# Four of the eight late modulation blocks moved into the feature stage of a planned one-core diffusion step, and the order of all engines set anew

## The chip, the cores and the metric

The kernel runs on one core of one Trainium2 chip. The metric is the device time of one execution in microseconds. It is taken as the median of several runs; lower is better.

## The reference

The reference is one inference step of one layer. 1024 latent tokens and 128 context tokens of width 1024 are normalised and modulated, projected once, and sent through two token mixers (HGRN2 with 4 heads of 128, RWKV-7 with 8 heads of 64, both in both directions). The results are joined, projected and added; then comes a gated feed-forward part with a depthwise convolution.

```python
mod = jax.nn.silu(c) @ ada_w[l] + ada_b[l]            # 6 sections of 1024, for c and for c_ctx
shift1, scale1, gate1, shift2, scale2, gate2 = jnp.split(mod[:, None, :], 6, axis=-1)
h = rmsnorm(x, p['norm_mix_w']) * (1 + scale1) + shift1
u = h @ p['w_in']
o_a, s_hgrn_new = hgrn2_mixer(u[..., :P_A], ...)
o_b, s_rwkv_new = rwkv7_mixer(u[..., P_A:], ...)
x = x + gate1 * (jnp.concatenate([o_a, o_b], axis=-1) @ p['w_out'])
h = rmsnorm(x, p['norm_ffn_w']) * (1 + scale2) + shift2
gt = ffn_conv_fn(h @ p['ffn_w_gate']) + p['ffn_conv_b']
x = x + gate2 * ((jax.nn.gelu(gt) * (h @ p['ffn_w_up'])) @ p['ffn_w_down'])
```

What matters here is `mod`: a product of two rows (c and c_ctx) with a 1024 x 6144 matrix, 25 MB to load for little arithmetic. `shift1` and `scale1` are needed at once. `gate1`, `shift2`, `scale2` and `gate2`, columns 2048 to 6143, are needed only after the mixers. Scans that depend on every earlier token (RWKV-7) are computed in chunks of 64 tokens; a chunk needs the inverse of a triangular 64 x 64 system.

## The kernel before, in words

**Recording and planning.** The kernel does not issue its instructions as it is written. The class `Plan` records every operation (an `Op`: one instruction, or a group kept together) with what it reads and writes, and in `schedule` sets one order for TensorE (PE), VectorE (DVE), ScalarE (ACT), GpSimd (POOL) and SyncE (SP, which issues the loads; stores go to SP or POOL, whichever the plan picks). At each step it takes, for the engine that is free first, the ready operation with the highest rank: the length of the work that hangs on it (`tail`) plus a lead. Leads come from the table `LEADS` by the function that recorded the operation, and from `with plan.ahead(...)`. On PE a change between the split-precision matmuls (mode `f32r`) and all others costs rank (`INTO`, `OUT`, `SWITCH`). Costs of operations and transfers (`pe_cost`, `wire`) are numbers in the code. Places in memory are given out with the order: a tile's buffers are used in turn, and tiles that share a place (`near`) follow each other in the order of the program. Each engine and each queue then runs its list in order, so an instruction that waits holds up all behind it.

**Stages.** (1) The input is loaded, normalised and transposed; `mod_columns` makes `shift1` and `scale1`; the first two column blocks are projected (L1253 to L1255). (2) The feature stage: `conv_rkv` projects blocks of 128 columns by `proj` (each product is a triple of `f32r` matmuls, L1098 to L1100, of 128 x 384), `features` makes the chunk matrices of one of four head pairs, and `elim` inverts the triangular systems on DVE, 31 steps of two instructions (L1478, L1481), then fills them up with small matmuls (L1497, L1506). It runs five times, for the four pairs and for the context. Its buffers are `asys`, `tsys` (loaded with identities, L1472), `etmp`, `ttd` and `tn`. (3) The chain stage: `chains` runs 18 dependent chunk steps for each of two groups of heads (loads at L1727 and L1729, values at L1736 and L1737, products at L1746, L1790, L1797, L1805 to L1818); `hgrn_block` (L1601 to L1662) and `hgrn_out` (L1692 to L1707) work beside them, the rest of the projections too, and toward its end the loads of the output weights (L1939) begin. (4) `wo_tile` (L1981 to L1983), (5) the feed-forward front (L2090), and (6) its second product `ffn_down` (L2239 to L2241).

**The modulation blocks.** `ada_block(b)`, b from 0 to 7, makes 512 columns: a bias row (L995), eight loads of 128 x 512 (256 KB each, L1002), for each load four matmuls with 32 columns of the stationary side (L1005; four more for the bias at L999), a copy (L1006), a store for blocks 0, 1 (`gate1`, read again by `gate_rows` before stage 4) and 6, 7 (`gate2`, read at stage 6), and a transpose (L1013). Blocks 2, 3 are `shift2` and 4, 5 `scale2`, needed in stage 4. The weights go through two buffers `adaw2`; all eight blocks are recorded in the loop over the chain steps, one for two steps, with the lead `LEAD_ADA`, the last two with 700.

In the profile an ordinary fp32 matmul leaves two records: one block has 64 at L1005, 8 at L999 and 1 at L1013.

Of the kernel before, what the change touches and what calls it, by code (L numbers as in the profile page):

```python
# [20 lines left out]
P = 128  # L21
# [10 lines left out]
NLATE = 5  # L32
FILL = (1, 1, 1)
STRETCH = 2.76
LEAD_ADA = -9.0
LATE = 1.2
SWITCH = 2.0
INTO = 3.22
OUT = 2.0
HAM = 3.413  # L40
QUIET = 0.65
BUSY = 200.0
LEADS = {'hgrn_block': -10.8, 'hgrn_out': 89.1, 'ada_block': 34.8, 'prep': 35.0, 'mod_scale': 90, 'const': 103.8, 'params': -82, 'param_loads': -0.4, 'wo_tile': 8.1, 'ffn_down': -27.1, 'chains': -3.8, 'hgrn_in': 0.0, 'features': 0.0, 'elim': -12.5, 'post': 22.1, 'conv_rkv': 0.0, 'bonus_rows': -40.6, 'turned': 0.0, 'step_kernel': 0.0}


C_W0, C_A0, C_KK, C_KA, C_RK, C_LNW, C_LNB = 0, 8, 12, 16, 20, 24, 28
# [125 lines left out]
class Plan:  # L172
# [147 lines left out]
    def close(self, forms, room=()):  # L320
        op = Op()
        op.id, op.forms, op.deps, op.succ, op.after = len(self.ops), forms, set(), [], []
        self.ops.append(op)
        reads, writes, op.tiles = [], [], set()
        for m, a, k, _ in forms[0][1]:
            w, r = self.operands(m, a, k)
            writes += w
            reads += r
        for ap in reads + writes + list(room):
            if ap.offset >> self.BITS:  # L330
                op.tiles.add(ap.offset >> self.BITS)
# [12 lines left out]

        todo = []
        for k, reg, whole in each(reads, False):
            ws, rs = self.live.setdefault(k, ([], []))
            for w in ws:
                if overlap(w[0], reg):
                    op.deps.add(w[1])  # L350
            todo.append((rs, reg))
        for k, reg, whole in each(writes, True):
            ws, rs = self.live.setdefault(k, ([], []))
            for l in (ws, rs):
                keep = []
# [12 lines left out]
        if self.first is not None:  # L368
            op.deps.add(self.first)
        for v in op.tiles:  # L370
            self.tiles[v][3] += 1
        op.place, op.dense, op.lead, op.kind = None, False, self.lead + LEADS.get(self.kind, 0.0), self.kind
# [107 lines left out]
    def wire(self, a):  # L480

        def run(x):
            r = 1
            for s, c in reversed(list(x.ap)[1:]):
                if c > 1 and s != r:
                    break
                r *= c
            return r
        total = a[0].ap[0][1] * self.count(a[0])
        piece = min(run(a[0]), run(a[1]), 16384)  # L490
        return total / piece * (.007 + .0371e-3 * 4 * piece) / 16 + .01

    @staticmethod
    def pe_cost(l):
        busy = [[0.0] * 4 for _ in range(4)]
        issue, mode = 0.0, None
        for m, a, k, _ in l:
            out, lhsT, rhs = a[0], a[1], a[2]
            q = lambda ap: ((ap.offset & Plan.LOW) // ap.ap[0][0]) // 32
            span = lambda n: 1 if n <= 32 else 2 if n <= 64 else 4  # L500
            if m == "transpose":
                rows, cols, r0, c0, t = span(lhsT.ap[0][1]), 4, q(lhsT), 0, .0048 + .00081 * Plan.count(lhsT)
            else:
                rows, cols, r0, c0 = span(lhsT.ap[0][1]), span(Plan.count(lhsT)), q(lhsT), q(out)
                n = Plan.count(rhs)
                if lhsT.dtype == F32R:
                    t = (n + 32) / 2400
                else:
                    t = 2 * max(.098 if cols == 4 else .052, .005 + .00083 * n)
            cells = [(i, j) for i in range(r0, min(4, r0 + rows)) for j in range(c0, min(4, c0 + cols))]  # L510
# [20 lines left out]
    def schedule(self):  # L531
# [106 lines left out]
        while done < len(ops):  # L638
# [54 lines left out]
            c = op.cost[e]  # L693
            if e == "PE":
                if mode is not None and op.mode != mode:
                    c += .12 if op.mode == "f32r" else .09
                mode = op.mode
                w = int(t / HAM)
                if area.get(w - 1, 0.0) < .4 * HAM:
                    c *= 1.9  # L700
                for v in range(w, int((t + c) / HAM) + 1):
                    area[v] = area.get(v, 0.0) + op.area * (min(t + c, (v + 1) * HAM) - max(t, v * HAM)) / c
                recent.append((t, t + c, op.area))
# [91 lines left out]
def step_kernel(ctx: ExitStack, tc: tile.TileContext, I, O):  # L795
# [52 lines left out]
    def banks(name, first, count, each=1, free=False):  # L848
# [17 lines left out]
        .add("kb", 768, 2).add("vt", 384, 2) \  # L866
        .add("ako", 1024).add("asys", 1024).add("tsys", 1024).add("etmp", 256).add("ttd", 1024) \
        .add("tn", 1024)
    Layout(fx, 0, NX).add("tt", 2048).add("wlora", 512).add("ha", 384, 2).add("hb", 384, 2)
    v0 = plan.tags["rkv"].places[0][1]  # L870
    plan.tag("sgt", [(low, v0 + 3 * T)], T)
# [66 lines left out]
    def pbank(tag="pj"):  # L938
        return tl(tag, [P, 512])
# [50 lines left out]

    def ada_block(b):

        c0 = 2048 + 512 * b
        br = tl("adab", [4, P])
        ld(br, I["ada_b"][0, c0:c0 + 512].rearrange("(a b) -> a b", b=P))  # L995
        ps, mr = pbank("a"), tl("adam", [P, P])
        with plan.together(mr):
            for q in range(4):
                mm(ps[32 * q:32 * q + 32, 0:P], one[:, q, :], br, True, False)  # L999
        for kt in range(KT):  # L1000
            w = tl("adaw2", [P, 512])
            ld(w, I["ada_w"][0, kt * P:(kt + 1) * P, c0:c0 + 512])  # L1002
            with plan.together():
                for q in range(4):
                    mm(ps[32 * q:32 * q + 32, 0:P], sT[:, kt, :], w[:, P * q:P * q + P], False, kt == KT - 1)  # L1005
# [6 lines left out]
        pq = pbank("a")  # L1012
        pe.transpose(pq[:, 0:P], mr, ident)  # L1013
# [533 lines left out]
    def conv_rkv(p, j):  # L1547
        t = tl("rkv", [P, T])
        conv_tiles((2560 + j * 512 + p * P, 4 * j + p, t))
        return t  # L1550

    kv = [conv_rkv(0, 1), conv_rkv(0, 2)]
    for p in range(NPAIR):
        k, v = kv
# [326 lines left out]
    def post(i, oh, ol, early):  # L1881
# [23 lines left out]
                pe.transpose(ps[:, p * P:(p + 1) * P], y[:, p * P:(p + 1) * P], ident)  # L1905
        split(oh[:, 4:8], ol[:, 4:8], ps.rearrange("p (k t) -> p k t", k=4))

    cg = [chains(0), chains(1)]
    rest = [(hgrn_block, h, tb) for h in range(4) for tb in range(3)]
    for n in range(NCH + 1):  # L1910
        for g in range(2):
            next(cg[g], None)
        if n % 2 == 0 and n:
            if n // 2 <= 8:
                with plan.ahead(700.0 if n // 2 > 6 else LEAD_ADA):
                    ada_block(n // 2 - 1)
        if n % 2 and n // 2 < NT:
            bonus_rows(n // 2)
# [416 lines left out]
```

## Time and profile before

| | |
|---|---|
| median of 3 runs | 1864.29 us (1860.72 to 1865.18) |
| profiled execution | 1861.02 us, its span 1859.2 us, mean granted clock of TensorE 0.989 |
| busy, share of the span | PE 96%, weight loads of PE 86%, DVE 76%, ACT 47%, POOL 16% |
| moved by the DMA queues | 307 MB, 165 GB/s over the span |

The span is cut below into stretches by the first matmul of a stage: the chains' first (L1746) starts at 535.4 us, the feed-forward front's first (L2090) close to 1071 us. A busy PE is not one at its peak, since ends of matmuls are modelled; so the idle time before an instruction and what ended it are read beside the busy share.

### The profile page before, as it was taken

To read this page: it belongs to the slowest core of one execution; us is meant where nothing else is said; L and a number is where in the kernel's file an instruction comes from. 1 tells how busy PE (TensorE), PEld (TensorE's weight loads), DVE (VectorE), ACT (ScalarE), POOL (GpSimd) and SP (SyncE) were. 2 spreads that over 40 slices of the span, in tenths; PEclk is the share of its full clock that TensorE was granted. 3 is DMA by queue.
4 is the path that set the end of the run, shared out by engine and by line. 5 is a ranking of instruction groups with operands and counts; after the bars stand their busy time and mean duration, and the time that the engine had idled before them with its cause. 6 is when DMAs were issued, how large, how long until landed. Compare 5 with 4: busy or idle time off the path is not lost.

```text
span 1859.2 us, 45181 instructions
## 1 busy us (share of the span) xinstructions
PE 1790.9 (96%) x18369; PEld 1602.7 (86%) x18369; DVE 1409.0 (76%) x2643; ACT 870.2 (47%) x1766; POOL 295.9 (16%) x565
## 2 busy tenths in 40 slices
PE   7999999999999998999899989999999999999998
PEld 4989888889987887888778889999999999887886
DVE  7659898977747787787787789999999954886443
ACT  6556666643235564655435854444444333422321
POOL 2113425353211221222100100000000000000000
PEclk9999999999999999999899989999999999999999
DMA  9325637486567678877977612222222246675351
GB/s 322 100 76 141 151 97 193 108 229 182 170 199 233 200 217 242 245 230 244 301 232 249 222 54 72 82 72 72 72 72 72 83 140 213 237 245 190 125 165 62
DMA packets 268927, 307.44 MB, mean 165 GB/s; under 512 B 62339, under 2 KB 213153, under 8 KB 268720
## 3 DMA queue, kind: packets, MB, share of 16 engines
q1 hardware_dynamic: 241568, 222.17, 40.4%
q0 software_dynamic: 27152, 82.40, 13.1%
q8 instruction: 144, 2.36, 0.5%
q14 instruction: 63, 0.52, 0.1%
HBM read 200.50 MB, written 103.99 MB: 164 GB/s over the span
## 4 chain that ended last, share of the span: by engine, by line
PE 69%; DMA 4%; DVE 2%; issue 1%; ACT 1%; ACTq 0%; DVEq 0%; SPq 0%
PE banks L2090 27%; PE banks L2239 5%; PE banks L2240 5%; PE banks L2241 5%; PE banks L1098 3%; PE banks L1099 3%; PE banks L1100 3%; PE banks L1746 2%; PE banks L1981 2%; PE banks L1983 2%; PE banks L1982 2%; DMA top<-in_ada_w_dram 2%; DMA low<-d_ak 1%; PE banks L1816 1%; PE banks L1790 1%
## 5 line engine op out<-in xcount | busy, mean ns | idle before, releaser
L1098 PE MATMUL banks<-hh,wh 128*128 128x384 f32 x768 | 278.3, 362 | 0.0
L1099 PE MATMUL banks<-hl,wh 128*128 128x384 f32 x768 | 258.3, 336 | 0.7 <-issue 0.7
L1100 PE MATMUL banks<-hh,wl 128*128 128x384 f32 x768 | 258.5, 337 | 0.0
L2179 DVE SCALAR_TENSOR_TENSOR low<-low,pf 128x1024 f32<-128x1024 f32 x176 | 224.7, 1278 | 6.8 <-ACT low L2173 5.3
L2090 PE MATMUL banks<-qm,wh 128*128 128x320 f32 x968 | 224.3, 311 | 0.0
L2090 PE MATMUL banks<-qm,wl 128*128 128x320 f32 x528 | 163.8, 310 | 2.3 <-DVE wl L2060 2.3
L2090 PE MATMUL banks<-hbm,wh 128*128 128x256 f32 x880 | 162.4, 282 | 0.0
L2090 PEld LDWEIGHTS banks<-qm,wh 128*128 128x128 f32 x968 | 162.2, 190 | 0.1
L1098 PEld LDWEIGHTS banks<-hh,wh 128*128 128x128 f32 x768 | 144.9, 189 | 19.6 <-issue 12.9
L1099 PEld LDWEIGHTS banks<-hl,wh 128*128 128x128 f32 x768 | 145.4, 189 | 3.3 <-issue 2.2
L1100 PEld LDWEIGHTS banks<-hh,wl 128*128 128x128 f32 x768 | 144.9, 189 | 0.0
L2090 PEld LDWEIGHTS banks<-hbm,wh 128*128 128x128 f32 x880 | 139.5, 190 | 0.0
L2090 PE MATMUL banks<-ham,wh 128*128 128x256 f32 (+1 forms) x616 | 133.3, 297 | 3.3 <-ACT ham L2023 2.5
L2090 PE MATMUL banks<-hbm,wl 128*128 128x256 f32 x440 | 124.3, 283 | 0.0
L2090 PEld LDWEIGHTS banks<-ham,wh 128*128 128x128 f32 x616 | 102.8, 192 | 3.7 <-ACT ham L2023 2.8
L2090 PEld LDWEIGHTS banks<-qm,wl 128*128 128x128 f32 x528 | 99.6, 189 | 2.6 <-DVE wl L2060 2.6
L2060 ACT CAST wh<-fx 128x512 fp32r<-128x512 f32 x88 | 54.5, 621 | 82.2 <-PE banks L2090 72.5
L2128 ACT COPY fx<-banks 128x320 f32<-128x320 f32 (+1 forms) x132 | 52.4, 397 | 81.7 <-PE banks L2090 81.4
L2239 PE MATMUL banks<-qm,hbm 128*128 128x512 f32 x216 | 85.5, 396 | 0.0
L2240 PE MATMUL banks<-qm,hbm 128*128 128x512 f32 x216 | 85.5, 396 | 0.0
L2241 PE MATMUL banks<-qm,hbm 128*128 128x512 f32 x216 | 85.4, 395 | 0.0
L2090 PEld LDWEIGHTS banks<-hbm,wl 128*128 128x128 f32 x440 | 84.0, 191 | 0.0
(510 smaller groups left out, 4368.8 us busy)
## 6 DMA issues: line engine op xcount, KB each, us to landing
wr<-in_w_in_dram SPq DMA_DIRECT2D x34, 512.0 KB
top<-in_ada_w_dram SPq DMA_DIRECT2D x64, 256.0 KB
low<-d_ak SPq DMA_DIRECT2D x64, 192.0 KB
d_a<-low POOLq DMA_DIRECT2D x21, 576.0 KB, 3.5
low<-in_ffn_w_up_dram SPq DMA_DIRECT2D x22, 512.0 KB
wr<-in_ffn_w_gate_dram SPq DMA_DIRECT2D x22, 512.0 KB
low<-d_kb SPq DMA_DIRECT2D x36, 256.0 KB
low<-d_a SPq DMA_DIRECT2D x12, 704.0 KB
```

The lines of the kernel that those rows point to most:

```text
L1098: mm(o, wh[:, kt, :], hh[:, kt, c], kt == 0, False)
L1099: mm(o, wh[:, kt, :], hl[:, kt, c], False, False)
L1100: mm(o, wl[:, kt, :], hh[:, kt, c], False, kt == KT - 1)
L1746: mm(pa[h][:, P * w:P * w + P], kb[hc[h], w, :], W[hc[h], A0[h] + 192 * w:A0[h] + 192 * w + P], True, True)
L1981: mm(ps, oh[:, kt, :], woh, kt == 0, False)
L2060: split(*w, src)
L2090: pe.matmul(o, a[:, kt, :], b[:, kt, :], start=start and first, stop=last, skip_group_check=not start)
L2128: act.copy(keep[n], y[:, 0:w])
L2179: dve.scalar_tensor_tensor(av, shifted(dy, dx), tap(3 * dy + dx), av, MUL, ADD)
L2239: mm(o, lh, w[:, 0, c], first, False)
L2240: mm(o, lh, w[:, 1, c], False, False)
L2241: mm(o, ll, w[:, 0, c], False, last)
```

## The change

Blocks 4 to 7 are recorded ahead of the feature stage, with buffers of their own: six for the weights in the places of `ttd`, `tn` and `tsys`, the bias row and the copy in that of `etmp`, and the PSUM banks `el` of the eliminations. Blocks 0 to 3 stay in the loop over the chain steps, with their two buffers. The planner's prices of transfers and of mode changes, its leads and the ranks `INTO`, `OUT` and `BUSY` are other numbers, and a table `NUDGE` adds a number to the lead of the operations of some groups of 64. No computation is added or left out. Line numbers after the change are 4 to 14 higher: L1005 becomes L1015, L1098 becomes L1108, L1746 becomes L1759.

```diff
+EARLY = (4, 5, 6, 7)
+LEAD_EARLY = -1.6
+LEAD_LAST = 300.0
-INTO = 3.22
-OUT = 2.0
+INTO = 4.2
+OUT = 1.36
-BUSY = 200.0
+BUSY = 186.0
+NUDGE = {1: -6, 2: 2, 3: 10, 12: -10, 13: -10, ...}
...
-        return total / piece * (.007 + .0371e-3 * 4 * piece) / 16 + .01
+        return total / piece * (.0085 + .0434e-3 * 4 * piece) / 16 + .01
...
-                    c += .12 if op.mode == "f32r" else .09
+                    c += .2 if op.mode == "f32r" else .1
...
+    at = {t: plan.tags[t].places[0][1] for t in ("tsys", "etmp", "ttd", "tn")}
+    plan.tag("adaw3", [(top, at[t] + 512 * b) for t in ("ttd", "tn", "tsys") for b in range(2)], 512)
+    plan.tag("adab3", [(top, at["etmp"])], 128)
+    plan.tag("adam3", [(top, at["etmp"] + 128)], 128)
...
-        c0 = 2048 + 512 * b
-        br = tl("adab", [4, P])
+        c0, early = 2048 + 512 * b, b in EARLY
+        br = tl("adab3" if early else "adab", [4, P])
...
-        ps, mr = pbank("a"), tl("adam", [P, P])
+        ps, mr = pbank("el" if early else "a"), tl("adam3" if early else "adam", [P, P])
...
-            w = tl("adaw2", [P, 512])
+            w = tl("adaw3" if early else "adaw2", [P, 512])
...
+    with plan.ahead(LEAD_EARLY):
+        for b in EARLY:
+            ada_block(b)
     kv = [conv_rkv(0, 1), conv_rkv(0, 2)]
...
+    late = [b for b in range(8) if b not in EARLY]
...
-            if n // 2 <= 8:
-                with plan.ahead(700.0 if n // 2 > 6 else LEAD_ADA):
+            if n // 2 - 1 in late:
+                with plan.ahead(LEAD_LAST if n // 2 > 6 else LEAD_ADA):
                     ada_block(n // 2 - 1)
```

What this does to the lists of the engines is seen at three places. The first is SP's list behind the loads of `shift1` and `scale1`, at the start of the feature stage; `wr` is the one buffer for projection weights, `in_ada_w` the modulation weights. Before:

```order
L1305 DMA wr<-in_w_in_dram 128x8x128
L1328 DMA low<-in_rwkv_g_dram 96x512
L1472 DMA top<-in_k_id_dram 128x1024
L1299 DMA fx<-in_rwkv_a_dram 32x512
L1298 DMA fx<-in_rwkv_w_dram 32x512 x2
L1295 DMA top<-in_k_smask_dram 128x390
L1524 DMA d_ak_78<-fx 256x1x32 x4
L1305 DMA wr<-in_w_in_dram 128x8x128 x4
```

Now (L1012 is the weights' load, L1315 that of the projection):

```order
L1315 DMA wr<-in_w_in_dram 128x8x128
L1012 DMA top<-in_ada_w_dram 128x512 x2
L1338 DMA low<-in_rwkv_g_dram 96x512
L1005 DMA top<-in_ada_b_dram 4x128
L1012 DMA top<-in_ada_w_dram 128x512
L1309 DMA fx<-in_rwkv_a_dram 32x512
L1308 DMA fx<-in_rwkv_w_dram 32x512 x2
L1012 DMA top<-in_ada_w_dram 128x512 x3
L1305 DMA top<-in_k_smask_dram 128x390
L1534 DMA d_ak_78<-fx 256x1x32 x3
L1315 DMA wr<-in_w_in_dram 128x8x128 x2
L1012 DMA top<-in_ada_w_dram 128x512 x3
```

Nine of the 32 early loads now stand among the first projections' weights, and the identities for the first elimination (L1472, third row before) have moved behind all 32.

The second place is PE's list in the features of the first head pair, where the small matmuls of `features` (L1380, L1390) begin to break into the triples. Before:

```order
L1380 MATMUL banks<-hsum,top 128x2 x3
L1390 MATMUL banks<-c_ident,low 128x128 x3
L1098 MATMUL banks<-hh,wh_132 128x384
L1099 MATMUL banks<-hl,wh_132 128x384
L1100 MATMUL banks<-hh,wl_134 128x384
L1390 MATMUL banks<-c_ident,top 128x128 x3
```

Now, with the second early block (bias L1009, weights L1015):

```order
L1009 MATMUL banks<-top,one 32x128 x4
L1015 MATMUL banks<-top,sT 32x128 x12
L1108 MATMUL banks<-hh,wh_132 128x384
L1109 MATMUL banks<-hl,wh_132 128x384
L1110 MATMUL banks<-hh,wl_134 128x384
L1015 MATMUL banks<-top,sT 32x128 x4
L1390 MATMUL banks<-hsum,top 128x2 x3
L1400 MATMUL banks<-c_ident,low 128x128 x3
L1015 MATMUL banks<-top,sT 32x128 x4
L1400 MATMUL banks<-c_ident,top 128x128 x3
L1015 MATMUL banks<-top,sT 32x128 x4
```

The early block's matmuls stand for the most part where PE leaves the triples anyway. Over the whole list up to the chains' first product there are 202 changes between triples and other matmuls, where there were 196. The last early block ends behind 144 triples of L1108.

The third place is PE's list late in the chain stage. Before, block 5 ends (L1013), and block 6 begins between the chain's products, with block 7 still to come:

```order
L1790 MATMUL banks<-low 64x64 x16
L1013 MATMUL banks<-c_ident,top 128x128
L999 MATMUL banks<-top,one 32x128 x4
L1005 MATMUL banks<-top,sT 32x128 x4
L1797 MATMUL banks<-low 64x64 x8
L1005 MATMUL banks<-top,sT 32x128 x4
L1797 MATMUL banks<-low 64x64 x8
```

Now, at about the same point of the chains, block 2 ends and block 3 begins, the last of those that stayed:

```order
L1015 MATMUL banks<-top,sT 32x128 x8
L1773 MATMUL banks<-c_ident,low 128x128 x4
L1023 MATMUL banks<-c_ident,top 128x128
L1009 MATMUL banks<-top,one 32x128 x4
L1759 MATMUL banks<-low 128x128 x8
L1803 MATMUL banks<-low 64x64 x8
```

One block is left to do from here on, where two were. The blocks that stay have moved later in the list: block 0 begins before the chains and is spread over their first half, and blocks 1 to 3 stand in the second half, where blocks 4 to 7 stood.

More of the change, by code (lines that the diff above doesn't have):

```diff
@@ L37 @@
 SWITCH = 2.0
-INTO = 3.22
-OUT = 2.0
+INTO = 4.2
+OUT = 1.36
 HAM = 3.413
 QUIET = 0.65
-BUSY = 200.0
-LEADS = {'hgrn_block': -10.8, 'hgrn_out': 89.1, 'ada_block': 34.8, 'prep': 35.0, 'mod_scale': 90, 'const': 103.8, 'params': -82, 'param_loads': -0.4, 'wo_tile': 8.1, 'ffn_down': -27.1, 'chains': -3.8, 'hgrn_in': 0.0, 'features': 0.0, 'elim': -12.5, 'post': 22.1, 'conv_rkv': 0.0, 'bonus_rows': -40.6, 'turned': 0.0, 'step_kernel': 0.0}
+BUSY = 186.0
+NUDGE = {1: -6, 2: 2, 3: 10, 12: -10, 13: -10, 14: -10, 17: -5, 20: 33, 31: 9, 38: 17, 41: 4, 42: 3, 47: 56, 56: -9, 59: -2, 63: 5, 64: -11, 69: -20, 70: 1, 77: 20, 78: 20, 79: -4, 80: 20, 81: 4, 83: -8, 84: 20, 87: 31, 90: -3, 94: 10, 95: 29, 96: -9, 97: 10, 98: 30, 99: 10, 100: 20, 101: -10, 103: 1, 108: -10, 109: -3, 110: 2, 114: -3, 115: 15, 116: -9, 122: -2, 123: -2, 126: -12, 128: -14, 129: 11, 130: 10, 131: 10, 132: 10, 134: -31, 135: 8, 136: 10, 138: 40, 140: -19, 141: -8, 143: -10}
+LEADS = {'hgrn_block': -3.6, 'hgrn_out': 106.6, 'ada_block': 47.3, 'prep': 119.5, 'mod_scale': 90, 'const': 103.8, 'params': -71.6, 'param_loads': -28.9, 'wo_tile': 8.1, 'ffn_down': 21.7, 'chains': 18.7, 'hgrn_in': 0.0, 'features': 0.0, 'elim': -12.5, 'post': 12.6, 'conv_rkv': 0.0, 'bonus_rows': 5.2, 'turned': 2.4, 'step_kernel': -1.0}
 C_W0, C_A0, C_KK, C_KA, C_RK, C_LNW, C_LNB = 0, 8, 12, 16, 20, 24, 28
@@ L371, in close @@
             self.tiles[v][3] += 1
-        op.place, op.dense, op.lead, op.kind = None, False, self.lead + LEADS.get(self.kind, 0.0), self.kind
+        op.place, op.dense, op.lead, op.kind = None, False, self.lead + LEADS.get(self.kind, 0.0) + NUDGE.get(op.id // 64, 0), self.kind
         op.table = None
@@ L509, in pe_cost @@
                     t = 2 * max(.098 if cols == 4 else .052, .005 + .00083 * n)
+                    if rows == 2:
+                        t *= 1.28 if cols == 4 else 1.6
             cells = [(i, j) for i in range(r0, min(4, r0 + rows)) for j in range(c0, min(4, c0 + cols))]
@@ L1011, in ada_block @@
                 st(g2d[:, 512 * (b - 6) + P * q:512 * (b - 6) + P * q + P], mr[32 * q:32 * q + 2, :])
-        pq = pbank("a")
+        pq = pbank("el" if early else "a")
         pe.transpose(pq[:, 0:P], mr, ident)
```

## The prediction

> **What bounds the kernel now.** I read the page's span and slices first, then the busy time by stage, then what ended PE's idle time, then single pieces of the chain of waits.
>
> ```profile
> span 1859.2 us, 45181 instructions
> PE 1790.9 (96%) x18369; PEld 1602.7 (86%) x18369; DVE 1409.0 (76%) x2643; ACT 870.2 (47%) x1766; POOL 295.9 (16%) x565
> PE   7999999999999998999899989999999999999998
> PEclk9999999999999999999899989999999999999999
> DMA  9325637486567678877977612222222246675351
> ```
>
> PE is busy nearly everywhere. Its clock is lower only in slices 20 and 24, and slice 20 is the one after the start in which the DMA engines are full (9). So the question for each stage is whether PE has work or waits. The stretches answer it; their columns are the stretch, its length, busy time of PE, PEld, DVE, ACT and POOL, granted clock, DMA share and GB/s.
>
> ```profile
> 9.70:140.00 130.30, 125.54 (x796) 103.84 (x796) 85.33 (x181) 74.81 (x152) 21.90 (x50) 1.00 0.53 161
> 140.00:535.40 395.40, 389.24 (x4147) 357.12 (x4146) 316.83 (x644) 204.33 (x394) 145.78 (x263) 1.00 0.59 159
> 535.40:760.00 224.60, 209.33 (x4266) 175.58 (x4266) 169.77 (x435) 121.90 (x283) 45.80 (x90) 0.98 0.74 221
> 760.00:885.00 125.00, 117.63 (x2608) 101.73 (x2604) 96.79 (x239) 67.34 (x165) 32.88 (x66) 0.99 0.82 248
> 885.00:945.00 60.00, 50.04 (x742) 41.43 (x742) 44.99 (x101) 27.23 (x58) 6.97 (x14) 0.89 1.00 298
> 945.00:1069.40 124.40, 123.93 (x918) 101.40 (x916) 96.35 (x181) 73.22 (x164) 12.53 (x23) 1.00 0.68 228
> 1069.40:1092.90 23.50, 17.23 (x92) 16.29 (x92) 20.60 (x39) 15.62 (x31) 1.16 (x2) 0.78 0.08 33
> 1092.90:1859.20 766.30, 756.79 (x4809) 704.30 (x4807) 575.97 (x815) 280.70 (x514) 21.87 (x41) 1.00 0.37 122
> ```
>
> The feature stage (140 to 535.4) leaves PE idle for 395.4 - 389.2 = 6.2 us: PE bounds it, and the DMA engines are half empty. In the chain stage (535.4 to 1069.4) PE is idle for 15.3 + 7.4 + 10.0 + 0.5 = 33.1 us, and 10.0 of these fall into the 60 us in which the DMA engines are full at 298 GB/s. Behind 1092.9 PE bounds again.
>
> What ended the chain stage's idle time (who waits, for what: us, times, longest; the first pair for 535 to 1069, the second for 885 to 945):
>
> ```profile
> PEld banks L1005 <- DMA top<-in_ada_w_dram: 14.8, 14, 2.1
> PE banks L1005 <- DMA top<-in_ada_w_dram: 11.1, 11, 1.9
> ...
> PEld banks L1005 <- DMA top<-in_ada_w_dram: 10.1, 7, 2.0
> PE banks L1005 <- DMA top<-in_ada_w_dram: 8.1, 7, 1.5
> ```
>
> A third of the 33.1 us is PE waiting for modulation weights: 11.1 us, 8.1 of them where the DMA engines are full. The loads also delay others, as the chain of waits shows (start, length) with the copies of chain values on POOL:
>
> ```profile
> 708.99 7.69 DMA low<-d_v
> 885.29 7.58 DMA low<-d_ak
> 934.94 8.96 DMA top<-in_ada_w_dram
> ...
> POOL low L1737 <- DMA low<-d_v: 109.7, 24, 14.4
> ```
>
> **The change part by part.** The sum is made against the profiled execution, 1861.0 us (span 1859.2 and 1.8 around it). The median of the runs, 1864.3, lies 3.3 above; the same difference is applied to it.
>
> *1. Matmuls added to the feature stage.* What a block costs on PE is read where one ran unhindered:
>
> ```profile
> 539.66 0.42 PE L999 MATMUL banks<-top,one 4*32 4x128 f32 x8
> 540.01 0.65 PE L1005 MATMUL banks<-top,sT 128*32 128x128 f32 x16
> 540.58 0.44 PE L1098 MATMUL banks<-hh,wh 128*128 128x384 f32 x1
> 540.86 0.34 PE L1099 MATMUL banks<-hl,wh 128*128 128x384 f32 x1
> 541.04 0.33 PE L1100 MATMUL banks<-hh,wl 128*128 128x384 f32 x1
> ...
> L1005 PE MATMUL banks<-top,sT 128*32 128x128 f32 x512 | 25.1, 287 | 11.9 <-DMA top<-in_ada_w_dram 11.1 <-issue 0.8
> L1013 PE MATMUL banks<-c_ident,top 128*128 128x128 f32 x8 | 2.5, 308 | 0.0
> ```
>
> From start to start, 16 records of L1005 take 540.58 - 540.01 = 0.57 us; a block has 512 / 8 = 64, so 2.3. The bias takes 0.35, the transpose 0.3. One block is 2.9 us, four are 11.7. The first triple matmul behind them takes 0.28 instead of 0.18, so a change costs 0.1; the order has six changes more before the chains, 0.6. Nothing covers this, since PE is full: at most the 6.2 us idle, which belong to other waits. **+12.3.** Copies on ACT (one per block) and DVE (two) lie beside PE.
>
> *2. The same matmuls leave the chain stage.* PE's list is in order and 94% busy there, so they count fully: **-11.7.**
>
> *3. Waits for their weights.* Between none of the 11.1 us (the four blocks that stay meet the same queue) and all of it. The order puts block 3 whole and the end of block 2 where the end of 5, block 6 and the start of 7 waited 8.1 us, so about half goes: **-5.5.**
>
> *4. Bytes.* Of the modulation loads
>
> ```profile
> top<-in_ada_w_dram SPq DMA_DIRECT2D x64, 256.0 KB
> ```
>
> 32 leave, 8.4 MB. From 535.4 to 945 the rows give 221 x 224.6 + 248 x 125 + 298 x 60 = 98.5 MB, so 8.5% goes. The idle time that is left (33.1 - 11.1 = 22.0) stands largely before products that need chain loads. Bounds: 0, if those waits are latency and not bytes, and -22. The last chain steps and the output weights still share the queue with two blocks, so I stay nearer to nothing, at about a quarter: **-6.**
>
> *5. Clock.* The stage loses 0.02 x 224.6 + 0.01 x 125 + 0.11 x 60 = 12.3 us of PE's cycles. It falls with waits that are short:
>
> ```profile
> 885.00:912.00 27.00, 22.65 (x345) 18.67 (x345) 21.67 (x53) 14.84 (x30) 1.88 (x4) 0.81 0.98 305
> ```
>
> With a clock of 0.81 in these 27 us, the longest wait in the rows above is 2.0 us; shorter waits still must add up to save the clock. Bounds 0 and -12; a third, as of the idle time (11.5 of 33.1): **-4.** [...]
>
> *6. The first elimination starts later.* Its `tsys` can be loaded only when the last early block has been multiplied, and that stands behind 144 triples:
>
> ```profile
> 47.00:168.50 121.50, 52.17 (x144) 27.03 (x144) 1.00 0.42 115
> ...
> L1478 DVE TENSOR_TENSOR top<-top x155: 183/359/427, 161.9 to 486.2; 128x31 f32<-128x31 f32 x10, 128x60 f32<-128x60 f32 x10, 128x87 f32<-128x87 f32 x10, 128x112 f32<-128x112 f32 x10
> ```
>
> The first row counts L1098: its 144th ran by 168.5, with term 1 by some 180, so elimination begins near 183 and not at 161.9. DVE is idle for 395.4 - 316.8 = 78.6 us of the stretch, and the last step ended at 486.2, 49 us ahead of the chains. That covers 21 us: **0**, and up to +21 were the cover gone.
>
> *7. The new order elsewhere.* Behind the first L2090 the matmuls stand in the same order, and PE is 99% busy. At the passage into it (6.3 us idle, clock 0.78) ACT and DVE have been reordered; I have no row for the new order: **0**, within -6 and +6. SP's first loads keep their place; the start stays.
>
> Sum: 12.3 - 11.7 - 5.5 - 6 - 4 = **-14.9 us**. The execution would take 1846.1, the median **1849.4 us**. With terms 3 to 5 between half and one and a half times (8 to 23) the forecast's own range is 1841 to 1857.
>
> **The rivals.**
>
> *The full queue stays (no change).* The output weights, the last chain loads and `hgrn_out` keep the DMA engines full, blocks 2 and 3 take the place of 6 and 7, and terms 3 to 5 vanish: +0.6, that is 1865 (1857 to 1868). For it speaks the 1.00 in 885 to 945 and the third place of the order; against it that one block, 2.1 MB or 7 us at 298 GB/s, is gone from there, and three before.
>
> *SP's list stands still (slower).* The early loads have six buffers. A load that finds none stands in SP's list until PE has multiplied, and behind it stand the features' stores (`kb`, `v`) and projection weights; with two buffers for each stored tile, DVE and then PE stop. The place is the features of the first pair, 80 to 180 us. The price: eight loads in a row wait for matmuls spread over 21 triples, each 3 x 0.18 = 0.53 us from the rows above, so 11 us; with the next block the same, 22 in all. -14.9 + 22 = +7: **1871** (1868 to 1882). It turns to slower than before once PE's new idle time there is over 15 us. Against it: some stores go through POOL, and the stretch to 140 has the DMA engines half idle. [...]
>
> *All waits go (much faster).* The chain steps become evenly filled, and two thirds or more of 33.1 + 12.3 us go: 1826 to 1841, about 1834. For it: 945 to 1069 runs with 0.5 us idle at 228 GB/s. Against it: that stretch is mostly long matmuls, not chain steps.
>
> That the change does not do what it says is excluded: the lists show it.
>
> **How the numbers follow.** Forecast (1841 to 1857) 0.52; full queue 0.22; standing SP 0.16; much faster 0.10. A measurement of this kernel tells 0.3%, 5.6 us, from no change: below 1858.7 is faster, above 1869.9 slower. Faster: 0.52 + 0.10 + a quarter of 0.22 = 0.67; slower: 0.16 less what lies under 1869.9 = 0.14; the rest, 0.19, the same. The range 1835 to 1871 leaves out about half of each outer rival, 0.13 together, and takes in the bounds of terms 6 and 7 singly, but not all bounds at once.
>
> **What would show it.** In the profile afterwards: the first L1746 near 547.5 (term 1; over 560 means SP or the elimination); 32 loads of modulation weights within the first 180 us; PE's idle time in the chain stage near 22 us; PE's waits at the blocks' matmuls near 5.5; DMA share under 1.00 in the 60 us before the last chain steps, with a clock over 0.95; the first elimination step near 183. The prediction is wrong if the feature stage grows by more than the matmuls, or if the chain stage from first L1746 to first L2090 (536 us) is not shorter by 20 to 35.

## The result and the profile after

The changed kernel takes 1861.87 us (median of 12 runs, 1856.28 to 1871.98), the kernel before 1861.14 (12 runs, 1855.97 to 1865.18). The ratio is 1.0012, 95% interval 0.9996 to 1.0028: no change. The forecast was 1849.4 and faster, so it was wrong. Runs of one kernel spread over 9.2 us (before) and 15.7 us (changed) here and a profiled execution is one of them, so verdicts below go by ratios, and profiles by stage.

The page of the changed kernel, as read before:

```profile
span 1860.4 us, 45145 instructions
PE 1794.6 (96%) x18369; PEld 1605.7 (86%) x18369; DVE 1403.8 (75%) x2635; ACT 870.5 (47%) x1774; POOL 300.5 (16%) x568
PE   7999999999999999999899989999999999999998
PEclk9999999999999999999999989999999999999999
DMA  9447265466657677777986611222221245766351
```

Slice 20's clock is at 9 again, and the first slices move more. The same stretches as before, cut at this kernel's own first matmuls of the stages:

```profile
9.70:140.00 130.30, 125.74 (x905) 101.66 (x907) 80.67 (x179) 73.80 (x152) 22.69 (x52) 1.00 0.63 199
140.00:558.90 418.90, 409.05 (x4329) 371.72 (x4327) 320.36 (x650) 209.09 (x403) 150.45 (x272) 0.98 0.58 159
558.90:760.00 201.10, 190.34 (x4123) 163.64 (x4120) 164.13 (x416) 118.06 (x278) 44.24 (x84) 0.98 0.73 213
760.00:885.00 125.00, 118.07 (x2446) 100.32 (x2443) 96.51 (x246) 69.44 (x173) 30.17 (x59) 0.99 0.75 226
885.00:945.00 60.00, 53.14 (x893) 45.45 (x893) 39.95 (x89) 26.00 (x57) 9.76 (x18) 0.94 0.98 304
945.00:1069.80 124.80, 122.75 (x786) 100.96 (x786) 99.31 (x188) 71.56 (x161) 12.26 (x22) 1.00 0.70 230
1069.80:1095.50 25.70, 17.73 (x94) 16.41 (x93) 23.25 (x43) 16.80 (x33) 1.55 (x2) 0.80 0.14 53
1095.50:1860.40 764.90, 756.61 (x4809) 704.56 (x4808) 576.83 (x814) 280.42 (x514) 22.00 (x42) 1.00 0.37 122
```

Two large moves cancel. **The feature stage ends 23.5 us later** (558.9 against 535.4). PE idles 418.9 - 409.05 = 9.9 us in it, 3.7 more than before, and the clock has fallen from 1.00 to 0.98. These rows show where:

```profile
310.40:317.20 6.80, 6.80 (x77) 5.34 (x76) 6.67 (x12) 5.95 (x13) 5.65 (x10) 0.50 0.91 235
368.40:371.80 3.40, 3.31 (x12) 3.31 (x13) 3.33 (x8) 2.79 (x6) 0.96 (x2) 0.51 0.15 56
399.20:402.60 3.40, 3.40 (x11) 3.40 (x12) 2.00 (x4) 1.55 (x3) 2.29 (x5) 0.50 0.81 159
```

PE is full there at half its clock; 13.6 us at half clock lose 6.8. What is left, 23.5 - 3.7 - 6.8 = 13.0, is put down to the blocks' matmuls, 11.7 to 12.3 by the prediction's rows. **The chain stage is 23 us shorter** (510.9 from first L1759 to first L2104, against 533.5: before, the first L2090 runs at 1068.9, so the prediction's 536 for this stretch was 2.5 too long). Its idle time is 10.8 + 6.9 + 6.9 + 2.0 = 26.6 (33.1 before), and its clock loses 4.0 + 1.3 + 3.6 = 8.9 (12.3 before). The matmuls that left are the rest, 22.6 - 6.5 - 3.4 = 12.7 (good to about 1 us, since the rows give the clock with two digits). Behind it 1.7 us are lost at the passage and 1.4 won in the stretch behind, where a wait of 1.3 us at the start of `ffn_down` is gone.

Why the feature stage is long shows at the first elimination (L1488, its identities loaded at L1482, the early blocks' transposes at L1023, the chains' first product L1759; behind the shortest, median and longest duration in ns stand the first and the last start):

```profile
L1488 DVE TENSOR_TENSOR top<-top x155: 165/358/427, 185.7 to 509.3; 128x31 f32<-128x31 f32 x10, 128x60 f32<-128x60 f32 x10, 128x87 f32<-128x87 f32 x10, 128x112 f32<-128x112 f32 x10
...
  DMA top<-in_k_id_dram: 1.5, 1
...
L1482 SPq DMA_DIRECT2D top<-in_k_id_dram x5: 327/346/352, 181.9 to 456.3; - x5
...
L1759 PE MATMUL banks<-low x576: 267/272/579, 558.9 to 958.1; 64*128 64x128 f32 x192
```

The identities are loaded at 181.9, when the last early block is being multiplied (its transpose runs at 183.6), and DVE waits 1.5 us for them. The first step comes at 185.7, 23.8 us later than before, the last at 509.3, 23.1 later, and the chains' first product 23.5 later. None of the delay was absorbed. New idle time comes with it: PE's waits that DVE ended, from 140 us to the chains' first product, were 0.3 us before and are 4.8 now. The longest is at transposes of an HGRN2 input (L1285), until a step of an elimination has ended, at 449 us (in all, times, longest):

```profile
PE banks L1285 <- DVE top L1488: 2.4, 1, 2.4
```

Further on, the chain of waits (start, length) runs over SP's list. The second load of identities stands there until 230.3, when the first elimination is over, and a projection weight (`wr`) behind it lands late; PE waits 1.75 us at 247.2:

```profile
231.13 4.47 DMA d_ak<-top
235.60 10.12 DMA wr<-in_w_in_dram
245.77 1.05 issue
246.82 0.50 ACT fx L1289
```

### The profile page after: what moved, and what is told of

Same layout as the page of the kernel before. It is cut to its first block, busy times and chain, and to the rows that moved or that the text cites. A ratio compares the mean times of both kernels' runs of the same rounds, so it can differ in the third digit from the quotient of the medians.

```text
span 1860.4 us, 45145 instructions
## 1 busy us (share of the span) xinstructions
PE 1794.6 (96%) x18369; PEld 1605.7 (86%) x18369; DVE 1403.8 (75%) x2635; ACT 870.5 (47%) x1774; POOL 300.5 (16%) x568
## 4 chain that ended last, share of the span: by engine, by line
PE 82%; DMA 8%; DVE 5%; issue 2%; ACT 2%; POOL 1%; SPq 1%; DVEq 0%; ACTq 0%; POOLq 0%
PE banks L2104 27%; PE banks L1108 6%; PE banks L1109 5%; PE banks L1110 5%; PE banks L2253 5%; PE banks L2254 5%; PE banks L2255 5%; DMA low<-d_ak 2%; PE banks L1759 2%; PE banks L1995 2%; PE banks L1997 2%; PE banks L1996 2%; DMA top<-d_hu 1%; PE banks L1803 1%; PE banks L1829 1%
## 5 line engine op out<-in xcount | busy, mean ns | idle before, releaser
L1108 PE MATMUL banks<-hh,wh 128*128 128x384 f32 x768 | 280.3, 365 | 0.0
L2104 PE MATMUL banks<-qm,wh 128*128 128x320 f32 x968 | 224.6, 311 | 0.0
L2104 PE MATMUL banks<-qm,wl 128*128 128x320 f32 x528 | 163.7, 310 | 3.8 <-DVE wl L2074 3.8
L1108 PEld LDWEIGHTS banks<-hh,wh 128*128 128x128 f32 x768 | 146.0, 190 | 22.4 <-issue 14.3
L2104 PE MATMUL banks<-hbm,wh 128*128 128x256 f32 x880 | 163.1, 282 | 0.0
L2104 PEld LDWEIGHTS banks<-qm,wh 128*128 128x128 f32 x968 | 162.0, 190 | 0.1
L2104 PEld LDWEIGHTS banks<-hbm,wh 128*128 128x128 f32 x880 | 139.7, 190 | 0.0
L2104 PE MATMUL banks<-ham,wh 128*128 128x256 f32 (+1 forms) x616 | 133.8, 297 | 3.4 <-ACT ham L2037 3.0
L2104 PE MATMUL banks<-hbm,wl 128*128 128x256 f32 x440 | 124.4, 283 | 0.0
L2104 PEld LDWEIGHTS banks<-ham,wh 128*128 128x128 f32 x616 | 102.9, 192 | 3.9 <-ACT ham L2037 3.2
L2104 PEld LDWEIGHTS banks<-qm,wl 128*128 128x128 f32 x528 | 99.7, 189 | 4.1 <-DVE wl L2074 4.1
L2142 ACT COPY fx<-banks 128x256 f32<-128x256 f32 (+1 forms) x132 | 52.3, 397 | 84.5 <-PE banks L2104 83.5
L2203 POOL DMA_DIRECT2D d_a<-low x22 | 11.7, 532 | 464.5 <-DVE low L2202 255.7
```

Source lines behind the costliest of these rows:

```text
L1108: mm(o, wh[:, kt, :], hh[:, kt, c], kt == 0, False)
L2104: pe.matmul(o, a[:, kt, :], b[:, kt, :], start=start and first, stop=last, skip_group_check=not start)
L2142: act.copy(keep[n], y[:, 0:w])
```

## The experiments

Theory A: the early blocks keep the buffers of the inverses, the first elimination starts late, and the delay passes through to the end of the stage as idle PE and half clock. Theory B: the new numbers of the planner lengthen the feature stage, wherever the blocks stand.

### One half of the change alone, and other leads

x1_early_old_tables: the early blocks with the planner's old numbers.

```diff
-INTO = 4.2
-OUT = 1.36
-BUSY = 186.0
-NUDGE = {1: -6, 2: 2, 3: 10, ...}
+INTO = 3.22
+OUT = 2.0
+BUSY = 200.0
+NUDGE = {}
...
```

> The four early blocks stay; the numbers that set the order (leads, the per-part nudges, the prices of mode changes, transfers and two-row matmuls) are those of the kernel before. By its order the fourth early block's transpose stands behind 170 of the 768 triples of L1108 (144 with the change). Theory A (the early blocks keep the inverses' buffers until they are multiplied, the eliminations start late, and the delay comes back as idle TensorE and as bunched small matmuls at half clock): the first elimination starts later than with the change (185.7 us), near 205; the first chain matmul comes at 558 us or later, up to 580; time 1861 to 1885. Theory B (the new tables make the feature stage longer, not the blocks' place): the feature stage grows by the blocks' own 12 us only, first chain matmul near 548, time near 1851.

x2_late_new_tables: the new numbers, no early block.

```diff
-EARLY = (4, 5, 6, 7)
+EARLY = ()
```

> The new numbers stay, no block is early: all eight are in the chain stage as before. Theory A: first elimination near 162 us as before, first chain matmul within 4 us of the 535.4 before, no half-clock window between 140 us and it; the chain stage within 5 us of the 533.5 us before; time 1855 to 1868. Theory B: the feature stage is longer by about 11 us although nothing was put into it, first chain matmul near 546, and with a chain stage as before the time is near 1872.

x3_lead60 and x3_lead20: another lead for the early blocks.

```diff
-LEAD_EARLY = -1.6
+LEAD_EARLY = 60.0
```

> The change with one number edited: the lead of the early blocks is 60 instead of -1.6, which puts their fourth transpose behind 90 of the 768 triples of L1108 instead of 144 (near 128 us instead of 183.6). Theory A: the first elimination starts near 165 us, the first chain matmul comes at 548 to 551 (the blocks' own 12 us and little else), at most one half-clock window in the feature stage, and the time is about 10 us below the change's, near 1852. Theory B: the feature stage stays as long as with the change, first chain matmul near 559, time near 1862. A third way: the loads that are wanted earlier are waited for before 130 us, so that the first 96 triples end later than 146.3 us by as much as is won behind.

> The same with a lead of 20: the fourth transpose stands behind 107 triples (near 147 us). Theory A: first elimination near 165 to 170 us, first chain matmul 549 to 553, time near 1853. Theory B: as with the change, 559 and 1862.

All four are slower than before: 1883.74 us (ratio 1.0127, 1.0111 to 1.0142), 1882.58 (1.0115, 1.0091 to 1.0140), 1880.28 (1.0105, 1.0074 to 1.0136) and 1882.24 (1.0120, 1.0103 to 1.0138), the kernel before 1860.07. No expectation had the last three that slow. The two rows of the new numbers without early blocks, and those of the lead 60:

```profile
L1488 DVE TENSOR_TENSOR top<-top x155: 180/359/427, 162.4 to 494.9; 128x31 f32<-128x31 f32 x10, 128x60 f32<-128x60 f32 x10, 128x87 f32<-128x87 f32 x10, 128x112 f32<-128x112 f32 x10
L1759 PE MATMUL banks<-low x576: 272/272/579, 548.2 to 965.0; 64*128 64x128 f32 x192
```

```profile
L1488 DVE TENSOR_TENSOR top<-top x155: 170/361/568, 180.5 to 506.6; 128x31 f32<-128x31 f32 x10, 128x60 f32<-128x60 f32 x10, 128x87 f32<-128x87 f32 x10, 128x112 f32<-128x112 f32 x10
L1759 PE MATMUL banks<-low x576: 272/272/549, 557.8 to 967.3; 64*128 64x128 f32 x192
```

In x2 the feature stage is 12.8 us longer with nothing put into it, which is B's case. (Part of this is its own doing: `NUDGE` goes by the numbers of the operations, and without the early blocks' 96 operations it hits others.) In x3 the fourth early transpose ran at 145.4, yet the first elimination started at 180.5, because the planner had put 142 triples ahead of it. So the hold of the buffers is not the only thing that delays it; the written order is another. With the lead 20 the first elimination came at 180.3, the first chain product ahead of the last triples, so that its 515.8 cannot be compared. In x1 the elimination came at 202.0 and the chains' first product at 564.1, as A had it. The chain stage took 527 (x1), 541 (x2) and 535 us (x3 at 60). Each set of numbers fits one kernel: after each of these four edits the planner's order is worse by about 20 us, so these runs do not separate the theories as times.

### The four blocks taken out of an order that stays

In the next four kernels the planner works as ever, but marked instructions are not issued, so that the order of everything else is untouched. Blocks 4 to 7 then hold their biases only.

```diff
-            for op in self.order:
+            for op in [o for o in self.order if not (o.tiles & set(self.tags["adaw3"].made))]:
```

That is y2_after_no_four; y1_before_no_four takes `adaw2` from its 33rd tile on, and y3_after_no_matmuls and y4_before_no_matmuls ask for `o.forms[0][0] == "PE"` too, so that the loads stay.

> The kernel before, in its own order, with the weight loads and weight matmuls of blocks 4 to 7 left out (those four blocks hold only their biases; all else is computed). It is what the chain stage can win at most, with nothing put into the feature stage. Feature stage as before (first chain matmul near 535.4). If the forecast's terms for the chain stage are right (matmuls -11.7, their waits -5.5, fewer bytes -6, clock -4), first chain matmul to first L2090 falls from 533.5 to about 506 us and the time to about 1834. If what the bytes and the waits cost comes back as other waits: down by the matmuls and 5 us or so, near 516 us, time near 1844.

> The changed kernel, in its own order, with the weight loads and weight matmuls of the four early blocks left out. Theory A (the blocks and their hold on the inverses' buffers make the feature stage long): the first elimination comes before 170 us instead of at 185.7, the first chain matmul at 535 to 540 instead of 558.9, time near 1840. Theory B (the new order makes the feature stage longer whatever is in it): only the blocks' own 12 to 14 us go, first chain matmul at 545 to 547, half-clock windows still there, time near 1849.

> The changed kernel, in its own order, with only the weight matmuls of the four early blocks left out; their loads stay. If the matmuls and the hold of TensorE on the buffers are what costs, the time is that of the run without loads and matmuls. If the 32 loads themselves cost (SP's list, bytes in the feature stage), it is longer by what they cost: over 3 us.

> The kernel before, in its own order, with only the weight matmuls of blocks 4 to 7 left out; their loads stay in the chain stage. The difference to the run without both is what the 8.4 MB cost there when nothing waits for them: the forecast had 6 us (bounds 0 to 22). Expected time: near 1844 if fewer bytes and waits are worth what the forecast said, within 2 us of the run without both if bytes there are hidden.

Against 1859.87 for the kernel before: y1 1848.60 (0.9939, 0.9920 to 0.9957), y4 1857.78 (0.9990, 0.9970 to 1.0010), y2 1862.59 (1.0017, 0.9997 to 1.0036), y3 1865.10 (1.0046, 1.0023 to 1.0068).

**In the chain stage** the four blocks cost 11 us in all, where the forecast had 27. Without their matmuls alone the time is the same; their loads are worth 9 us more (1857.78 - 1848.60). Both missed what was expected, 1844 at most for y1 and 1844 or y1's own time for y4. The whole chain stages of y1 and y4:

```profile
538.20:1058.00 519.80, 489.54 (x8268) 412.91 (x8267) 407.14 (x954) 289.08 (x668) 97.77 (x192) 0.98 0.74 227
```

```profile
535.80:1065.00 529.20, 493.43 (x8270) 417.49 (x8267) 406.85 (x954) 288.70 (x668) 97.17 (x192) 0.97 0.77 239
```

y1 is 13.7 us shorter there than before. PE is idle for 519.8 - 489.5 = 30.3 us, against 33.1. The waits for modulation weights are gone but for 2.1 us (11.1 before), and others have come: PE's waits that DVE ended, summed over the stage, were 2.3 us before and are 8.8 in y1 and in the changed kernel. The largest of y1, with the weights' own:

```profile
PE banks L1746 <- DMA low<-d_ak: 4.8, 5, 2.1
...
PE banks L1695 <- DVE top L1678: 2.2, 2, 1.1
PE banks L1005 <- DMA top<-in_ada_w_dram: 2.1, 1, 2.1
...
PE banks L1705 <- DVE top L1701: 1.9, 2, 1.8
```

**In the feature stage** y2 gives no time back, though 32 loads and 128 matmuls are gone:

```profile
L1488 DVE TENSOR_TENSOR top<-top x155: 165/359/427, 182.4 to 506.4; 128x31 f32<-128x31 f32 x10, 128x60 f32<-128x60 f32 x10, 128x87 f32<-128x87 f32 x10, 128x112 f32<-128x112 f32 x10
L1759 PE MATMUL banks<-low x576: 272/272/373, 556.1 to 950.8; 64*128 64x128 f32 x192
```

The biases and transposes of the blocks still stand in their places (the fourth transpose runs at 181.9), so the hold and the order stay, and with them the elimination at 182.4 and the stage's end, 374 us later. So the blocks' matmuls alone do not decide in this order. (Part of what they would have given back, some 7 us, was lost to a stretch at half clock, shown in the last section.) Neither theory had foreseen it so: A expected the hold to go with the matmuls, and B had 12 to 14 us less. Whether the loads cost anything there (y3 is 2.5 us above y2) is not settled; the intervals overlap.

### Orders crossed

Theory D: a stage takes what its written order gives it, and the feature stage ends some 374 us behind its first elimination. For the last four kernels the order is written out: every engine gets its list from a table, and the planner only finds buffers and times.

```diff
-                if ready[e]:
-                    t = max(free[e], min(a for _, a in ready[e]))
+                can = [x for x in ready[e] if x[0].slot in (None, head[e])]
+                if can:
+                    t = max(free[e], min(a for _, a in can))
```

`slot` is an operation's place in its engine's table, `head` the next place to be served; the early blocks' operations have none in z1, z2 and z5, and are taken when they are ready (their loads from a given time on, one for each 1.6 us, 2.4 in z5) and PE is out of `f32r`. z1 takes both tables of the kernel before, z2 those of before up to the chains' first product and of the change from there, z3 the reverse.

> The order of the kernel before, instruction by instruction on every engine, with nothing changed but the four blocks: their loads go into SP's list from about 40 us on, their matmuls into TensorE's order at places where it is out of full-width mode anyway (the transposes stand behind 22, 45, 62 and 85 triples), and the one tsys load that would wait for their buffers stands behind them. Theory D (a stage has the time that its written order gives it; the blocks cost their matmuls in the feature stage and win 14 us in the chain stage): first chain matmul at 547 to 551, chain stage near 520 as in the run without the four blocks, time 1857 to 1862, no change. Theory A (the hold on the inverses' buffers costs): the blocks are done by 125 us, so the feature stage grows by the matmuls alone, as theory D has it too, but then the change's missing 11 us were the late place of its blocks. The forecast's terms for the chain stage: 506 us there, time near 1847.

> Up to the first chain matmul the order of the run above (order of before, with the four blocks put in early), from there on the order of the changed kernel, instruction by instruction. Theory D: first chain matmul at 547 to 551, chain stage near the 510.9 us of the change, first L2090 near 1060, time near 1851, about 10 us less than both kernels. If the chain stage's time hangs on what the feature stage leaves behind and not on its order: chain stage 515 to 521, time 1855 to 1860.

> The other way round: up to the first chain matmul the order of the changed kernel with its early blocks in their places, from there on the order of the kernel before. Theory D: first chain matmul near 559, chain stage near 520, first L2090 near 1079, time near 1870, about 0.5% slower than before. If the chain stage's gain comes from the blocks and not from its order: chain stage near 511, time near 1861.

> The fastest version so far (order of before up to the first chain matmul with the four blocks put in, then the order of the change), with nothing edited but the blocks' pace: their third and fourth transposes stand behind 72 and 104 triples instead of 62 and 85, and the first tsys load behind them. Theory A (the hold on the inverses' buffers is what costs in the changed kernel): first elimination some 10 us later, near 185 us as in the changed kernel, and the first chain matmul later by 5 to 10 us, at 554 to 559. Theory D without A (a later start of the eliminations is absorbed): first chain matmul at 547 to 551 again, time within 3 us of 1852.

| feature stage's order | chain stage's order | time, us | ratio to before | interval |
|---|---|---|---|---|
| before, blocks early (z1) | before | 1856.69 | 0.9996 | 0.9978 to 1.0015 |
| before, blocks early (z2) | change | 1852.20 | **0.9963** | 0.9945 to 0.9981 |
| change (z3) | before | 1870.27 | 1.0074 | 1.0052 to 1.0096 |
| change | change | 1861.87 | 1.0012 | 0.9996 to 1.0028 |
| before, blocks early but later (z5) | change | 1860.99 | 0.9983 | 0.9959 to 1.0008 |

The kernel before took 1859.14 beside z1 to z3, 1861.14 beside the change and 1863.51 beside z5, so rows are compared by their ratios. The first three came out as D had them, within 2 us; the profiled executions of z1 to z3 lie 2 to 10 us under their medians, with stages up to 6 us (z2's chain stage 8 us) shorter than D's. The change's feature order costs 0.8% with the one chain order and 0.5% with the other; its chain order wins 0.6% and 0.3%. Joined the better way they beat both kernels: z2 is 0.37% faster than before. Its feature stage, the chain stage and the two starts:

```profile
140.00:548.70 408.70, 402.50 (x4251) 367.54 (x4249) 329.06 (x666) 212.78 (x413) 150.63 (x272) 1.00 0.59 159
548.70:1051.90 503.20, 477.69 (x8234) 405.56 (x8230) 401.69 (x938) 285.08 (x666) 95.96 (x183) 1.00 0.76 234
```

```profile
L1488 DVE TENSOR_TENSOR top<-top x155: 185/360/427, 174.1 to 500.2; 128x31 f32<-128x31 f32 x10, 128x60 f32<-128x60 f32 x10, 128x87 f32<-128x87 f32 x10, 128x112 f32<-128x112 f32 x10
L1759 PE MATMUL banks<-low x576: 266/272/374, 548.7 to 940.1; 64*128 64x128 f32 x192
```

The blocks are done at 137, the first elimination starts 12.2 us later than before, the stage ends 13.3 later: the blocks' matmuls and one stretch of 3.4 us at half clock (1.7 us), with 6.2 us idle as before. (This execution took 1844.49, nearly the shortest of its 12 runs, so the rows flatter z2 by some 8 us.)

z5 moves the third and fourth block back by 10 and 19 triples:

```profile
L1488 DVE TENSOR_TENSOR top<-top x155: 185/359/428, 179.4 to 506.6; 128x31 f32<-128x31 f32 x10, 128x60 f32<-128x60 f32 x10, 128x87 f32<-128x87 f32 x10, 128x112 f32<-128x112 f32 x10
...
  DMA top<-in_k_id_dram: 3.9, 1
...
L1759 PE MATMUL banks<-low x576: 272/272/373, 555.8 to 955.5; 64*128 64x128 f32 x192
```

The elimination starts 5.3 us later than in z2 (DVE waits 3.9 us for its identities; A had some 10 later), and the stage ends 7.1 later, where A had 5 to 10 and "absorbed" would have had nothing. Executions of one feature order ended the stage within 4 us of each other (z2 548.7, z1 548.3; change 558.9, z3 554.9), so 7.1 stands out, if not by much. It is made up as in the change: the stage's idle time is 8.9 us (6.2 in z2), and 10.2 us run at half clock (3.4 in z2), which loses 3.4 more. The new idle time is one wait at 204 us, at a product of the next pair's features whose input DVE makes between steps of the elimination:

```profile
PE banks L1390 <- DVE top L1386: 3.2, 2, 2.9
```

As a time this is not settled: the intervals of z2 and z5 overlap.

Over the runs, from first elimination to the chains' first product in us: before 373.5, change 373.2, z1 372.8, z2 374.6, z3 371.1, z5 376.4, y1 375.5, y2 373.7, y3 376.0, y4 373.5, lead 60 377.3. Outside stand x1 (362.1) and x2 (385.8). In x1 the elimination starts 40.1 us later than before and the stage ends 28.7 later, so 11.4 us of the delay were made up; in x2 the start is the old one and the stage is longer. So some 374 us is what most of these orders gave, not a law. A's core, that the delay passes through, holds in the change and where one order's start was moved (z5); its cause is wider than the hold of the buffers.

How a late start is paid for can be counted in the triples of L1098 (L1108) ahead of the first elimination, for before, the change, z2 and z5:

```profile
68.50:161.90 93.40, 47.98 (x131) 24.42 (x131) 1.00 0.44 120
```

```profile
69.20:185.70 116.50, 53.49 (x148) 27.71 (x148) 1.00 0.57 172
```

```profile
68.60:174.10 105.50, 46.97 (x131) 24.40 (x130) 1.00 0.61 177
```

```profile
68.50:179.40 110.90, 49.23 (x139) 26.02 (x139) 1.00 0.60 173
```

The change spends 17 triples more, 17 x 0.53 = 9 us of PE's long work, before DVE has begun to invert. With the blocks' 13.0 that makes 22 of the 23.8 us. Behind it the eliminations take as long as ever (323.6 us from first to last step, 324.3 before). That those 9 us are then missing as filling between the small matmuls is the reading that fits: 3.7 us turn into idle time and 6.8 into half clock.

## Why the prediction was wrong, step by step

- *Matmuls added (+12.3):* right; 13.0, as what is left of the stage.
- *First elimination later, priced 0:* **the step that failed.** The start near 183 was right (185.7). "That covers 21 us" was not: the stage's end moved by 23.5, which is 10.5 beyond the blocks' matmuls, 3.7 of them idle time and 6.8 half clock (the bound given was 21). It is what the prediction had named as its sign of being wrong, a feature stage that grows by more than the matmuls. DVE's 78.6 us of idle time and the 49 us between the last step and the chains are no reserve. DVE's one list holds the elimination's steps among work that PE needs next. With a late start PE waits for DVE (0.3 us before, 4.8 in the change; 0.7 in z2, 3.4 in z5), and the projections that would have filled PE meanwhile have been spent. The waits are shown; that the spent projections cost idle time and clock is read from the triples and the half-clock stretches. z5, which delays the start within one order, supports both in the profile.
- *The same matmuls leave (-11.7):* 12.7 by the rows. But y4 shows that by themselves they bring no time that could be measured: PE's being "94% busy" in an ordered list did not make them count fully.
- *Waits for their weights (-5.5) and bytes (-6):* together -6.5 instead of -11.5. The waits fell by 10.3 us (11.1 to 0.8), nearly twice the forecast; others rose by 3.8, those that DVE ends from 2.3 to 8.8. y1 shows the same in the old order. The two terms were added as if what is late next cost nothing.
- *Clock (-4):* -3.4 in the chain stage, but 6.8 lost in the feature stage, which no term had.
- *Order elsewhere (0):* right within 2 us behind the chain stage; inside the two stages the order was worth as much as any other term (0.5 to 0.8% and 0.3 to 0.6%, z1 to z3).

The sum: +23.5 instead of +12.3 in the feature stage, -22.6 instead of -27.2 in the chain stage, with the passage +1.2 instead of -14.9 for the span. Of the rivals, "the full queue stays" had the right time for another reason: the DMA share is 0.98 in the last chain steps, but the chain stage did get shorter. The price of the standing SP list, 15 us of new idle time on PE, did not come (3.7). That 1861.87 lies inside the stated 1835 to 1871 is no credit to the mechanism: the range was wide enough for half of each outer rival. And the 3.3 us added for the median were scatter of three runs; over 12 the kernel before has 1861.14.

What stays open: how much of the missing gain in y1 (11 instead of 27 us) another order of the chain stage would fetch. The change's own order is worth 0.3% to 0.6% there.

## What to carry to other kernels

Here 78.6 us of slack on DVE, summed over a stage, did not pay for a start 23.8 us later of a serial line that recurs in it: the stage ended 23.5 us later. So ask which long work must stand between the steps of such a line, and whether the delay spends it early. To price work that is to be moved, leave it out of the old order and of the new one, with all else in place: two runs would have shown here that it is worth 11 us where it leaves, and that the place it goes to is held by something else. Where an order is fitted to a kernel, cross the orders stage by stage before judging the change; here the better half of each made the only complete version that is faster, by 0.37%.

## What the hardware showed unexpectedly

PE's clock halved here without idle time ahead of it. In the changed kernel, the 3.4 us before the first half-clock stretch, and what ran in them:

```profile
306.90:310.30 3.40, 3.40 (x76) 2.98 (x76) 2.77 (x5) 3.34 (x5) 2.45 (x5) 1.00 0.91 296
```

```profile
L1516 PE MATMUL banks<-top 32*32 32x32 f32 x64 | 2.0, 228 | 0.0
L1411 PE MATMUL banks<-low,fx 32*128 32x384 f32 x1 | 0.7, 709 | 0.0
L1390 PE MATMUL banks<-hsum,top 128*128 128x2 f32 x5 | 0.7, 251 | 0.0
```

PE is busy for 3.40 of 3.40 us, with small matmuls and transposes and no triple, and the next 6.8 us run at 0.50. (Busy by modelled ends; how much of PE these matmuls use, the profile does not say.) In the feature stage of the change the 3.4 us ahead of the three half-clock stretches (from 310.4, 368.4 and 399.2) hold 0, 3 and 5 single matmuls of triples, where at 0.18 us each some 19 would fit; ahead of 368.4 PE also idles, for 0.4 us. No threshold follows: 3.4 us with as few were followed by the full clock, from 160.1 in the change (5, with PE idle for 1.0 us) and from 368.3 in the kernel before (1, with PE busy throughout); the 3.4 us behind each of the two run at 1.00. Taking the blocks' matmuls away in y2 brought half clock too, there behind a wait of 1.9 us for DVE. The change first, then y2 and its wait:

```profile
121.50:135.20 13.70, 13.32 (x128) 9.35 (x127) 10.51 (x22) 6.67 (x14) 2.82 (x5) 1.00 0.84 288
```

```profile
121.50:135.20 13.70, 13.19 (x40) 10.17 (x41) 8.99 (x20) 6.04 (x13) 3.50 (x6) 0.50 0.18 53
...
L1390 PE MATMUL banks<-hsum,top 128*128 128x2 f32 x6 | 1.4, 356 | 1.9 <-DVE top L1386 1.9
```

Less work took the same time: 13.2 of 13.7 us busy at half clock, which loses 6.9 us, beside 13.3 at full. That is one reason why leaving out 13 us of matmuls brought nothing. The half-clock stretches are 6.8, 3.4 and 3.4 us long in the change and 13.7 in y2. Idle time alone does not account for them: ahead of 310.4 PE was busy for 3.40 of 3.40 us, and in y2 it idled for only 1.9 us. That the kind of matmul decides is a reading of these stretches; no run here tests it by itself.
